# Conditioning sums of layer 0 on VectorE instead of TensorE, beside a differential attention

## The chip, the cores and the metric

The kernel runs on one core of one Trainium2 chip. The metric is the device time of one launch in microseconds. The engines are TensorE (PE; PEld is its weight load), VectorE (DVE), ScalarE (ACT), GpSimd (POOL) and the queue of SyncE (SP), which issues most transfers.

## The reference, cut to what matters

The network has two layers on 128 context tokens and 1024 latent tokens of width 1024. Layer 0 is neighbourhood attention beside differential attention, layer 1 two recurrent mixers; a SwiGLU block follows each. The change touches the modulation that every layer computes from two conditioning vectors:

```python
def ada_modulation(cond, w, b):
    m = (jax.nn.silu(cond) @ w + b)[..., None, :]
    return jnp.split(m, 6, axis=-1)

m_ctx = ada_modulation(c_ctx, w_ada[layer], b_ada[layer])
m_lat = ada_modulation(c, w_ada[layer], b_ada[layer])
h_lat = modulate(rms_norm(lat, norm_mix_g[layer]), m_lat[0], m_lat[1])
...
lat = lat + m_lat[2] * mix_lat
lat = lat + m_lat[5] * swiglu(modulate(rms_norm(lat, norm_ffn_g[layer]), m_lat[3], m_lat[4]), w_ffn_in[layer], w_ffn_out[layer])
```

So two vectors of 1024 are multiplied with a 1024 x 6144 matrix in each layer. The first two of the six parts are needed before the layer's projections, the other four only after its mixer. The work beside it in layer 0 is the differential attention:

```python
s = jnp.einsum('bqhcd,bkhcd->bhcqk', qb, k).astype(jnp.float32) * scale
p = jax.nn.softmax(s, axis=-1)
p = (p[:, :, 0] - lam * p[:, :, 1]).astype(v.dtype)
return jnp.einsum('bhqk,bkhe->bqhe', p, v)
```

## The kernel before, in words

Tokens are held as nine tiles of 128. Large products are made in three matmuls each, high part times high, high times low and low times high, from float32r halves (`split`, L73 and L74: a cast on ACT, a subtraction on DVE).

`norm_input` loads and transposes x, computes the first four 512-column groups of the modulation (`ada`, L175, float32 matmuls straight from the loaded blocks), and writes the normalized input as `hH` and `hL`. Before that last step it calls `ahead`, which opens the pool `wpool` and starts the projection of the first head group.

`attn` then has a stage for the differential attention, of four heads with nine query tiles each. `pipe` goes through the 36 units; a unit has seven pieces: `a` (load q, rope, transpose: L434 and L427 on DVE, L437 on POOL, L488), `b0` and `b1` (scores of either half, L558 and L559; row maxima on DVE, L560 and L562; exponentials on ACT, L564; sum, L568; in `b1` the combination of the halves, L581) and four pieces `c` (transposes of the probabilities, L516, copies `pT`, L518, products with V, L522). Pieces of three successive units are interleaved by the list `order`. After each piece `fill` pulls 0.28 of a step from each of two generators: `gs`, the projections of the other seven head groups (`proj_tok`, L390 to L392, result copied at L408), and `ada`, the other eight 512-column groups of layer 0's modulation.

`ada` is `ada_steps(0, range(4, 12), wpool, ps)`. A step takes one of eight blocks of 128 x 512 of a group: `ada_load` (L132, 256 KB on SP's queue, two `aw` buffers), `ada_split` (cast `awh` on ACT, L139; subtraction `awl` on POOL, L140; three buffers each) and `ada_mm` (two matmuls with the four columns of `cond`, high and low parts of both vectors, L147). Loads run three steps ahead and splits two. After eight steps `ada_end` copies the four partial rows to SBUF (L155), turns them with four small matmuls that also add high and low part (`comb`, L159), and `ada_mod` adds the bias on DVE (L169).

PSUM has eight banks. In this stage `psAB` has one `mm`, two `S`, two `T` and one `o`; `psA` has one more `S` and the bank `ada`. `_Mux` hands out score banks in the turn "bba". The `mm` bank serves the projections and the small matmuls of `ada_end`.

Layer 1's modulation is already computed in another way, by `ada_vec` beside the first SwiGLU block: DVE multiplies each block with one element per partition and accumulates into `aacc` (L221, L223), for either vector; after eight steps eight float32 matmuls with a column of ones (L229) add over the partitions, into an `mm` bank.

The order of instructions on each engine is fixed when the kernel is built: the framework's scheduler takes the program's order as priority, lets later work run ahead where its buffers are free, and places instructions by a planned timeline.

Of the kernel before, what the change touches and what calls it, by code (L numbers as in the profile page):

```python
# [12 lines left out]
F32R = mybir.dt.float32r  # L13
I32 = mybir.dt.int32
AF = mybir.ActivationFunctionType
ALU = mybir.AluOpType
AX = mybir.AxisListType
PSUM = bass.MemoryType.PSUM
DRAM = bass.MemoryType.DRAM

P = 128
# [22 lines left out]
class Net:  # L44
# [41 lines left out]
    def setup(self, top):  # L86
        tc, nc, I = self.tc, self.nc, self.I
        self.const = top.enter_context(tc.tile_pool(name="const", bufs=1))
        self.dram = top.enter_context(tc.tile_pool(name="dram", bufs=1, space=DRAM))
        c = self.const  # L90
        self.ident = self.t(c, [P, P], tag="ident")
        nc.sync.dma_start(self.ident, I["k_ident"])
        self.ones = self.t(c, [P, 1], tag="ones")
        nc.vector.memset(self.ones, 1.0)
        self.epsc = self.t(c, [P, 1], tag="epsc")
        nc.vector.memset(self.epsc, EPS)
        self.v1 = self.t(c, [P, P], tag="v1")
        self.v2 = self.t(c, [P, 44], tag="v2")
        with tc.tile_pool(name="vst", bufs=1) as p, tc.tile_pool(name="vps", bufs=2, space=PSUM) as ps:
            r1 = self.t(p, [P, P], tag="r1")  # L100
            r2 = self.t(p, [44, P], tag="r2")
            nc.scalar.dma_start(r2[0:8], I["c_ctx"].rearrange("(r p) -> r p", p=P))
            nc.scalar.dma_start(r2[8:16], I["c"].rearrange("a (r p) -> (a r) p", p=P))
            nc.scalar.dma_start(r1[0:96], I["b_ada"].rearrange("l (r p) -> (l r) p", p=P))
            nc.scalar.dma_start(r1[96:112], I["norm_mix_g"].rearrange("l (r p) -> (l r) p", p=P))
            nc.scalar.dma_start(r1[112:128], I["norm_ffn_g"].rearrange("l (r p) -> (l r) p", p=P))
            nc.gpsimd.dma_start(r2[16:24], I["rw_w0"].rearrange("a d (r p) -> (a d r) p", p=P))
            nc.gpsimd.dma_start(r2[24:32], I["rw_a0"].rearrange("a d (r p) -> (a d r) p", p=P))
            nc.gpsimd.dma_start(r2[32:36], I["rw_k_k"].rearrange("a (r p) -> (a r) p", p=P))
            nc.gpsimd.dma_start(r2[36:40], I["rw_k_a"].rearrange("a (r p) -> (a r) p", p=P))  # L110
            nc.gpsimd.dma_start(r2[40:44], I["rw_r_k"].rearrange("a (r h) k -> (a r) (h k)", h=2))
            nc.scalar.activation(r2[0:16], r2[0:16], AF.Silu)
            pt = self.t(ps, [P, 512], tag="pt")
            nc.tensor.transpose(pt[:, 0:44], r2, self.ident[0:44, 0:44])
            nc.vector.tensor_copy(self.v2, pt[:, 0:44])
            pt = self.t(ps, [P, 512], tag="pt")
            nc.tensor.transpose(pt[:, 0:128], r1, self.ident)
            nc.vector.tensor_copy(self.v1, pt[:, 0:128])
        self.cond = self.t(c, [P, KT, 4], F32R, tag="cond")
        cv = self.v2[:, 0:16].rearrange("p (c k) -> p k c", c=2)  # L120
        self.split(self.cond[:, :, 0::2], self.cond[:, :, 1::2], cv)
        self.comb = self.t(c, [4, 2], tag="comb")
        nc.scalar.dma_start(self.comb, I["k_comb"])
        self.mod = [[None] * 6, [None] * 6]
        for l in range(2):
            for j in range(6):
                self.mod[l][j] = self.t(c, [P, KT, 2], tag=f"mod{l}{j}")
# [4 lines left out]
        self.nc.sync.dma_start(w, src[:, k : k + n, cg * 512 : (cg + 1) * 512])  # L132
        return w

    def ada_split(self, w, n, pool, eng=None):
        nc = self.nc
        wh = self.t(pool, [P, n, 512], F32R, tag="awh")
        wl = self.t(pool, [P, n, 512], F32R, tag="awl")
        nc.scalar.copy(wh, w)  # L139
        (eng or nc.gpsimd).tensor_tensor(wl, w, wh, op=ALU.subtract)  # L140
        return wh, wl

    def ada_mm(self, pt, k, n, ws):
        wh, wl = ws
        for i in range(n):
            for ww in (wh, wl):
                self.nc.tensor.matmul(  # L147
                    pt[0:4, :], lhsT=self.cond[:, k + i, :], rhs=ww[:, i, :], start=k + i == 0 and ww is wh, stop=k + i == KT - 1 and ww is wl
                )

    def ada_end(self, l, cg, pt, pool, ps, r=4):

        nc = self.nc
        s4 = self.t(pool, [r, 512], tag="as4", bufs=1)
        nc.scalar.copy(s4, pt[0:r, :])  # L155
        p2 = self.t(ps, [P, 512], tag="mm")
        comb = self.comb if r == 4 else self.ident[0:2, 0:2]
        for f in range(4):
            nc.tensor.matmul(p2[:, 2 * f : 2 * f + 2], lhsT=s4[:, f * P : (f + 1) * P], rhs=comb, start=True, stop=True)  # L159
        self.ada_mod(l, cg, p2)  # L160

    def ada_mod(self, l, cg, p2):
# [12 lines left out]
    def ada(self, l, cg, pool, ps, n):  # L175

        pt = self.t(ps, [P, 512], tag="mm")
        cond = self.v2[:, 0:16].rearrange("p (c k) -> p k c", c=2)
        for k in range(0, KT, n):
            w = self.ada_load(l, cg, k, n, pool)  # L180
            for i in range(k, k + n):
                self.nc.tensor.matmul(pt[0:2, :], lhsT=cond[:, i, :], rhs=w[:, i - k, :], start=i == 0, stop=i == KT - 1)
        self.ada_end(l, cg, pt, pool, ps, 2)

    def ada_steps(self, l, cgs, pool, ps, eng=None):

        seq = [(cg, k) for cg in cgs for k in range(KT)]
        raw, spl, pt = {}, {}, None
        for i in range(-3, len(seq)):
            if i + 3 < len(seq):  # L190
                raw[i + 3] = self.ada_load(l, *seq[i + 3], 1, pool)
            if 0 <= i + 2 < len(seq):
                spl[i + 2] = self.ada_split(raw.pop(i + 2), 1, pool, eng)
            if i >= 0:
                cg, k = seq[i]
                if k == 0:
                    pt = self.t(ps, [P, 512], tag="ada")
                self.ada_mm(pt, k, 1, spl.pop(i))
                if k == KT - 1:
                    self.ada_end(l, cg, pt, pool, ps)  # L200
                yield

    def ada_vec(self, l, cgs, pool):

# [1532 lines left out]
    def run(self):  # L1737
        tc, nc, I = self.tc, self.nc, self.I
        self.tail = iter(())
        with ExitStack() as top:  # L1740
            self.setup(top)
            self.qkv = [self.dram.tile([TOK, GW], F32, name=f"qkv{g}") for g in range(8)]
            self.odr = [self.dram.tile([TOK, P], F32, name=f"odr{g}") for g in range(8)]

            hp = tc.alloc_tile_pool(name="h0", bufs=1, side="right", reuse_waits="tile")
            hH, hL = self.tiles(hp, KT, "hH", F32R), self.tiles(hp, KT, "hL", F32R)
            wes = ExitStack()

            def ahead():
                wp = wes.enter_context(self.pool("wA", side="right"))  # L1750
                self.wpool = _Bufs(wp, {"wraw": 3, "wh": 9, "wl": 9, "ist": 2, "aw": 2, "awh": 3, "awl": 3})
                self.first = self.attn_in(0, hH, hL, self.wpool)
                next(self.first)

            self.norm_input(0, hH, hL, ahead)
            self.rpb_setup()
            self.diff_lam()
            xp, x, np_, hp, hH, hL = self.attn(hp, hH, hL, wes)
            self.dump("x0", x)
            self.ffn_block(0, x, hp, hH, hL, np_)  # L1760
            self.dump("x1", x)

            self.rec_setup()
            self.rec_proj(hH, hL, x, xp, np_)
            self.rec_scan(hp)
            xp, x = self.xp, self.x1
            np_, hp, hH, hL = self.rec_out(x)
            self.dump("x2", x)
            self.ffn_block(1, x, hp, hH, hL, np_)
            self.dump("x3", x)  # L1770
            xp.release()

    def attn(self, hp, hH, hL, wes):
# [20 lines left out]
        bp = _Bufs(both.enter_context(self.pool("kAB")), {"K": 2, "Q": 3, "pT": 2, "qraw": 2, "kraw": 2})  # L1794
        head = {}
        with ExitStack() as es:
            ps = _Mux(_Bufs(es.enter_context(self.pool("psA", space=PSUM)), {"S": 1, "ada": 1}), bps, ("mm", "T", "o"), {"S": "bba"})

            rp, vp, pp, op = (es.enter_context(self.pool(f"dA{i}")) for i in range(4))
            dp = _Route(_Bufs(pp, {"P": 3}), {"rm1": rp, "rm2": rp, "V": _Bufs(vp, {"V": 2}), "ob": op, "oss": op, "rs0": op, "rs1": op, "rs2": op}, bp)  # L1800
# [1 line left out]
            self.sin = self.t(rp, [P, 8, P], tag="sin")  # L1802
            nc.scalar.dma_start(self.cos, I["k_cos"].rearrange("(n p) c -> p n c", p=P))
            nc.scalar.dma_start(self.sin, I["k_sin"].rearrange("(n p) c -> p n c", p=P))
            ada = self.ada_steps(0, range(4, 12), wpool, ps)
            self.nps = _Turns(ps, ("mm", "S", "T"))
            fin(self.first)
            self.nps = ps
# [158 lines left out]
def consts():  # L1967
# [24 lines left out]
    for w in range(4):  # L1992
        for i in range(16):
# [2 lines left out]
            pat[k] = far  # L1996
            pat[k, :, cs : cs + 16] = 0.0
            sel[k, w::4, :, i] = 1.0
    comb = np.array([[1, 0], [1, 0], [0, 1], [0, 1]], f)
    i, j = np.arange(P)[:, None], np.arange(P)[None, :]  # L2000
    scan = np.stack([np.concatenate([i < j, i <= j], 1), np.concatenate([i > j, i >= j], 1)]).astype(np.int32)
    mE, mO = [], []
# [13 lines left out]
        "k_ret": ret,  # L2016
        "k_rkd": np.concatenate([P - 1 - i, i], 1).astype(f),
    }
    return {**extra, "k_comb": comb, "k_ident": ident, "k_cos": cos, "k_sin": sin, "k_namask": nam}


_INS = [
# [29 lines left out]
```

## Time and profile before

| what | value |
| --- | --- |
| median of 3 runs | 3992.53 us (3990.24 to 3998.9) |
| the profiled execution's own time | 3991.86 us |
| its span, first to last instruction | 3990.1 us |
| PE, DVE, ACT, POOL busy | 3790.7, 2169.5, 1250.4, 711.9 us |
| mean granted TensorE clock | 0.973 of full speed |

Busy time is the union of an engine's instructions. Matmuls are pipelined and their ends are modelled, so a row's duration of a matmul is longer than its distance to the next one. "Idle before" is time in which an engine had nothing to run just before the instruction named, followed by what ended it.

### The profile page before, as it was taken

What the parts mean: (1) busy time and instruction counts of PE and PEld (TensorE: products, weight loads), DVE (VectorE), ACT (ScalarE), POOL (GpSimd) and SP (SyncE); (2) the same over time, 40 slices, a digit from 0 to 9 for tenths busy, and PEclk for the clock granted to TensorE, in tenths of its full rate; (3) what the DMA queues carried; (4) which work ended last, traced back from release to release, by engine and by line L of the source; (5) the groups of instructions that cost most, each with busy time, mean ns of one, the idle gap of its engine ahead of it and who ended that gap; (6) DMA issues with size and microseconds to landing.
All of it is one profiled execution on the core that took longest, in us unless ns stands there. A gap on an engine that the chain in (4) does not pass through costs nothing.

```text
span 3990.1 us, 62872 instructions
## 1 busy us (share of the span) xinstructions
PE 3790.7 (95%) x23989; PEld 3559.6 (89%) x23989; DVE 2169.5 (54%) x5159; ACT 1250.4 (31%) x2930; POOL 711.9 (18%) x730
## 2 busy tenths in 40 slices
PE   8999997999999999998999998888888999999998
PEld 5899997999999999998989876776777999999998
DVE  5666665666454545345254656888875543343343
ACT  4555545555111111115232322233222411111112
POOL 3321202202100000012011232233322300000000
PEclk9999998999999999999999997999999999999999
DMA  6533316432222222213243434222223211111111
GB/s 203 150 105 91 95 52 163 126 85 88 67 80 64 85 64 80 69 46 116 87 129 102 163 123 142 66 70 63 64 64 103 64 38 45 41 37 43 43 40 53
DMA packets 378086, 339.98 MB, mean 85 GB/s; under 512 B 65428, under 2 KB 328720, under 8 KB 376248
## 3 DMA queue, kind: packets, MB, share of 16 engines
q1 hardware_dynamic: 359344, 324.37, 27.0%
q10 hardware_dynamic: 13160, 7.27, 0.7%
q0 software_dynamic: 5280, 4.31, 0.5%
q8 instruction: 190, 3.11, 0.3%
q14 instruction: 112, 0.92, 0.1%
HBM read 263.37 MB, written 72.38 MB: 84 GB/s over the span
## 4 chain that ended last, share of the span: by engine, by line
PE 78%; DVE 10%; DMA 5%; issue 3%; ACT 2%; POOL 1%; SPq 0%; ACTq 0%; DVEq 0%; POOLq 0%
PE mm L81 17%; PE mm L83 17%; PE mm L82 17%; PE o L522 3%; PE mm L390 2%; PE mm L392 2%; PE mm L391 2%; PE T L516 1%; DVE MB L1241 1%; DVE tf L1240 1%; PE mm L857 1%; PE A L1190 1%; PE mm L859 1%; PE mm L858 1%; PE S L558 1%
## 5 line engine op out<-in xcount | busy, mean ns | idle before, releaser
L81 PE MATMUL mm<-hH,wh 128*128 128x384 f32 x2544 | 865.1, 341 | 20.2 <-DVE nv L363 12.6
L82 PE MATMUL mm<-hL,wh 128*128 128x384 f32 x2544 | 860.6, 339 | 2.5 <-DVE hL L366 2.5
L83 PE MATMUL mm<-hH,wl 128*128 128x384 f32 x2544 | 859.8, 339 | 0.0
L769 DVE SCALAR_TENSOR_TENSOR x<-mm,mod,x 128x384 f32<-128x384 f32 (+2 forms) x896 | 431.5, 512 | 197.5 <-PE mm L83 195.8
L81 PEld LDWEIGHTS mm<-hH,wh 128*128 128x128 f32 x2544 | 480.0, 189 | 31.4 <-ACT wh L73 18.8
L82 PEld LDWEIGHTS mm<-hL,wh 128*128 128x128 f32 x2544 | 480.1, 189 | 5.6 <-DVE hL L366 2.7
L83 PEld LDWEIGHTS mm<-hH,wl 128*128 128x128 f32 x2544 | 480.0, 189 | 4.0 <-issue 2.9
L1692 POOL TENSOR_TENSOR gl<-fs,gh 128x384 fp32r<-128x384 f32 x132 | 140.4, 1063 | 1484.1 <-ACT gh L1691 1484.1
L74 DVE TENSOR_TENSOR wl<-wraw,wh 128x512 fp32r<-128x512 f32 (+2 forms) x360 | 217.9, 618 | 336.0 <-ACT wh L73 306.4
L82 PE MATMUL mm<-gl,owh 128*128 128x384 f32 x1056 | 353.0, 334 | 0.0
L83 PE MATMUL mm<-gh,owl 128*128 128x384 f32 x1056 | 352.9, 334 | 0.0
L81 PE MATMUL mm<-gh,owh 128*128 128x384 f32 x1056 | 350.4, 335 | 0.0
L1690 DVE TENSOR_TENSOR fs<-fs,mm 128x384 f32<-128x384 f32 x132 | 73.0, 553 | 430.3 <-PE mm L83 424.7
L73 ACT CAST wh<-wraw 128x512 fp32r<-128x512 f32 (+2 forms) x360 | 188.2, 530 | 205.5 <-DMA wraw<-in_w_ffn_in_dram 77.3
L73 ACT CAST owh<-owraw 128x1024 fp32r<-128x1024 f32 x60 | 62.9, 1049 | 489.7 <-PE mm L82 446.0
L390 PE MATMUL mm<-wh,hH 128*128 128x384 f32 x576 | 199.3, 346 | 3.8 <-ACT ist L408 3.7
L82 PEld LDWEIGHTS mm<-gl,owh 128*128 128x128 f32 x1056 | 198.3, 188 | 0.1
L83 PEld LDWEIGHTS mm<-gh,owl 128*128 128x128 f32 x1056 | 198.2, 188 | 0.0
L81 PEld LDWEIGHTS mm<-gh,owh 128*128 128x128 f32 x1056 | 197.8, 188 | 0.3 <-DVE x L769 0.3
L391 PE MATMUL mm<-wl,hH 128*128 128x384 f32 x576 | 195.3, 339 | 0.0
L392 PE MATMUL mm<-wh,hL 128*128 128x384 f32 x576 | 194.0, 338 | 0.0
L1689 ACT ACTIVATE fs<-mm 128x384 f32<-128x384 f32 x132 | 64.9, 492 | 383.5 <-PE mm L83 383.4
(385 smaller groups left out, 7437.8 us busy)
## 6 DMA issues: line engine op xcount, KB each, us to landing
wraw<-in_w_ffn_in_dram SPq DMA_DIRECT2D x352, 128.0 KB
aw<-in_w_ada_dram SPq DMA_DIRECT2D x160, 256.0 KB
owraw<-in_w_ffn_out_dram SPq DMA_DIRECT2D x44, 512.0 KB
F<-stg SPq DMA_DIRECT2D x34, 640.0 KB
stg<-st SPq DMA_DIRECT2D x12, 1536.0 KB
qkv<-ist SPq DMA_DIRECT2D x72, 192.0 KB
wraw<-in_w_in_attn_dram SPq DMA_DIRECT2D x64, 192.0 KB
nab<-rpbd SPq DMA_DIRECT2D x64, 192.0 KB
```

Of the source, the lines that this page charges most:

```text
L73: nc.scalar.copy(hi, src)
L74: nc.vector.tensor_tensor(lo, src, hi, op=ALU.subtract)
L81: mm(out, lhsT=wh, rhs=xh, start=first, stop=False)
L82: mm(out, lhsT=wh, rhs=xl, start=False, stop=False)
L83: mm(out, lhsT=wl, rhs=xh, start=False, stop=last)
L390: mm(pt[:, :ncol], lhsT=hH[k][:, c], rhs=WH[k], start=k == 0, stop=False)
L391: mm(pt[:, :ncol], lhsT=hH[k][:, c], rhs=WL[k], start=False, stop=False)
L392: mm(pt[:, :ncol], lhsT=hL[k][:, c], rhs=WH[k], start=False, stop=k == KT - 1)
L522: nc.tensor.matmul(o, lhsT=pT[:, i * P : (i + 1) * P], rhs=vs(b + i), start=b + i == 0, stop=b + i == nk - 1)
L769: self.nc.vector.scalar_tensor_tensor(x[f][:, c], pt[:, a:b], self.mod[l][jg][:, f, cd : cd + 1], x[f][:, c], op0=ALU.mult, op1=ALU.add)
L1690: nc.vector.tensor_tensor(s, s, pg[1][:, :GW], op=ALU.mult)
L1692: nc.gpsimd.tensor_tensor(gl[:, sl], s, gh[:, sl], op=ALU.subtract)
```

## The change

The eight later groups of layer 0 go through `ada_vec`, as layer 1's do: two DVE operations per block, then eight float32 matmuls with the column of ones per group. `ada_split`, `ada_mm`, `ada_steps`, `cond` and `comb` are gone, with the buffers `awh`, `awl` and the bank `ada`; that bank becomes a second `S` bank of `psA`, and score banks are handed out in the turn "ba", four in rotation. `ada_end` keeps only its form for two rows, which `norm_input` uses. The pulls of 0.28 and the order list stay.

```diff
-        self.cond = self.t(c, [P, KT, 4], F32R, tag="cond")
-        cv = self.v2[:, 0:16].rearrange("p (c k) -> p k c", c=2)
-        self.split(self.cond[:, :, 0::2], self.cond[:, :, 1::2], cv)
-        self.comb = self.t(c, [4, 2], tag="comb")
-        nc.scalar.dma_start(self.comb, I["k_comb"])
...
-    def ada_split(self, w, n, pool, eng=None):
...
-    def ada_mm(self, pt, k, n, ws):
...
-    def ada_end(self, l, cg, pt, pool, ps, r=4):
+    def ada_end(self, l, cg, pt, pool, ps):
...
-    def ada_steps(self, l, cgs, pool, ps, eng=None):
...
-                self.wpool = _Bufs(wp, {"wraw": 3, "wh": 9, "wl": 9, "ist": 2, "aw": 2, "awh": 3, "awl": 3})
+                self.wpool = _Bufs(wp, {"wraw": 3, "wh": 9, "wl": 9, "ist": 2, "aw": 2})
...
-            ps = _Mux(_Bufs(es.enter_context(self.pool("psA", space=PSUM)), {"S": 1, "ada": 1}), bps, ("mm", "T", "o"), {"S": "bba"})
+            ps = _Mux(_Bufs(es.enter_context(self.pool("psA", space=PSUM)), {"S": 2}), bps, ("mm", "T", "o"), {"S": "ba"})
...
-            ada = self.ada_steps(0, range(4, 12), wpool, ps)
+            ada = self.ada_vec(0, range(4, 12), wpool)
```

The function that takes over, unchanged:

```python
    def ada_vec(self, l, cgs, pool):
        nc = self.nc
        seq = [(cg, k) for cg in cgs for k in range(KT)]
        raw, acc = {}, None
        for i in range(-1, len(seq)):
            if i + 1 < len(seq):
                raw[i + 1] = self.ada_load(l, *seq[i + 1], 1, pool)
            if i < 0:
                continue
            cg, k = seq[i]
            w = raw.pop(i)[:, 0, :]
            if k == 0:
                acc = self.t(pool, [P, 2, 512], tag="aacc", bufs=1)
            for c in range(2):
                s = self.v2[:, c * 8 + k : c * 8 + k + 1]
                if k == 0:
                    nc.vector.tensor_scalar_mul(acc[:, c, :], w, s)
                else:
                    nc.vector.scalar_tensor_tensor(acc[:, c, :], w, s, acc[:, c, :], op0=ALU.mult, op1=ALU.add)
            if k == KT - 1:
                p2 = self.t(self.nps, [P, 512], tag="mm")
                for f in range(4):
                    for c in range(2):
                        o = p2[:, 2 * f + c : 2 * f + c + 1]
                        nc.tensor.matmul(o, lhsT=acc[:, c, f * P : (f + 1) * P], rhs=self.ones, start=True, stop=True)
                self.ada_mod(l, cg, p2)
            yield
```

## Rows read from the trace of the kernel before

**Rows 1.** The page's first part: busy time, share of the span, instructions.

```profile
PE 3790.7 (95%) x23989; PEld 3559.6 (89%) x23989; DVE 2169.5 (54%) x5159; ACT 1250.4 (31%) x2930; POOL 711.9 (18%) x730
```

**Rows 2.** Table by stage: length, PE, PEld, DVE, ACT, POOL busy (instructions), clock, DMA share, GB/s.

```profile
100.00:505.00 405.00, 392.77 (x2476) 368.07 (x2475) 257.33 (x618) 220.13 (x652) 107.83 (x94) 0.99 0.37 109
505.00:600.00 95.00, 94.55 (x628) 93.07 (x627) 59.24 (x162) 43.25 (x146) 3.23 (x7) 1.00 0.17 54
600.00:700.00 100.00, 77.23 (x483) 70.00 (x481) 48.88 (x143) 53.10 (x143) 21.89 (x32) 0.81 0.64 164
```

**Rows 3.** Groups from 100 to 505 us: busy us, mean ns, idle before and releaser.

```profile
L140 POOL TENSOR_TENSOR awl<-aw,awh 128x512 fp32r<-128x512 f32 x61 | 85.6, 1412 | 121.0 <-ACT awh L139 102.0 <-PE ada L147 18.8
...
L139 ACT CAST awh<-aw 128x512 fp32r<-128x512 f32 x61 | 37.5, 623 | 41.2 <-DMA aw<-in_w_ada_dram 38.6 <-PE ada L147 2.5
...
L147 PE MATMUL ada<-awh,cond 128*4 128x512 f32 x64 | 25.6, 399 | 0.7 <-ACT as L155 0.6 <-ACT awh L139 0.2
L147 PE MATMUL ada<-awl,cond 128*4 128x512 f32 x64 | 25.5, 398 | 1.8 <-POOL awl L140 1.8
...
L437 POOL TENSOR_TENSOR rm<-rm,rm 128x128 f32<-128x128 f32 (+1 forms) x33 | 22.7, 687 | 194.6 <-DVE rm L427 117.8 <-ACT P L564 34.0 <-PE mm L392 21.0
```

**Rows 4.** Table by stretch of L139 alone: length, ACT busy (casts), clock, DMA.

```profile
328.00:352.00 24.00, 4.98 (x8) 1.00 0.47 130
352.00:397.00 45.00, 0.00 (x0) 1.00 0.26 77
```

**Rows 5.** Waits, 100 to 505 us: total us, times, longest us.

```profile
DVE sm L568 <- ACT P L564: 58.1, 39, 5.0
...
ACT awh L139 <- DMA aw<-in_w_ada_dram: 38.6, 25, 3.2
```

**Rows 6.** Timeline near 350 us: start, duration, instruction, idle before and releaser.

```profile
346.86 0.62 ACT L139 CAST awh<-aw 128x512 fp32r<-128x512 f32 x1 [3.18 <-DMA aw<-in_w_ada_dram]
...
349.21 0.16 DVE L568 TENSOR_REDUCE sm<-mx 128x1 f32<-128x3 f32 x1 [2.38 <-ACT P L564]
...
349.93 1.40 DVE L581 SCALAR_TENSOR_TENSOR P<-P,r,P 128x1152 f32<-128x1152 f32 x1
...
351.38 0.66 PE L516 MATMUL T<-ident,P 128*128 128x128 f32 x4 [1.10 <-DVE P L581]
```

**Rows 7.** Timeline of PE near 281 us: first of three matmuls, and their successor.

```profile
281.02 0.40 PE L147 MATMUL ada<-awh,cond 128*4 128x512 f32 x1
...
281.72 0.60 PE L516 MATMUL T<-ident,P 128*128 128x128 f32 x4
```

**Rows 8.** Timeline of PE: one closing group of `ada_end`.

```profile
267.81 1.05 PE L159 MATMUL mm<-comb,as 4*128 4x2 f32 x8
```

**Rows 9.** Timeline of PE in layer 1's modulation: one closing group.

```profile
1021.36 1.84 PE L229 MATMUL mm<-ones,aacc 128*128 128x1 f32 x16
```

**Rows 10.** Timeline of DVE in layer 1's modulation: one pair of sums.

```profile
985.96 1.40 DVE L223 SCALAR_TENSOR_TENSOR aacc<-aw,v,aacc 128x512 f32<-128x512 f32 x2
```

**Rows 11.** Groups of DVE by shape, 100 to 505 us.

```profile
L581 DVE SCALAR_TENSOR_TENSOR P<-P,r,P 128x1152 f32<-128x1152 f32 x24 | 37.2, 1549 | 0.0
L74 DVE TENSOR_TENSOR wl<-wraw,wh 128x384 fp32r<-128x384 f32 x48 | 32.4, 687 | 8.9 <-ACT wh L73 8.7
```

**Rows 12.** Groups of DVE by shape, 505 to 600 us.

```profile
L581 DVE SCALAR_TENSOR_TENSOR P<-P,r,P 128x1152 f32<-128x1152 f32 x7 | 9.8, 1400 | 0.0
...
L74 DVE TENSOR_TENSOR wl<-wraw,wh 128x384 fp32r<-128x384 f32 x7 | 3.7, 555 | 1.0 <-ACT wh L73 0.9
```

**Rows 13.** Layer 1's `aacc`: what DVE waited for before its sums (us, times).

```profile
  DMA aw<-in_w_ada_dram: 31.1, 29
```

**Rows 14.** Table by stretch near the start; columns as in rows 2.

```profile
40.00:50.00 10.00, 7.00 (x19) 2.01 (x20) 6.99 (x19) 7.08 (x14) 2.73 (x3) 0.83 1.04 336
...
80.00:90.00 10.00, 8.83 (x52) 8.51 (x51) 1.29 (x2) 3.21 (x5) 0.00 (x0) 1.00 0.30 90
```

**Rows 15.** Timeline of PE: the first projection matmul.

```profile
63.13 0.44 PE L390 MATMUL mm<-wh,hH 128*128 128x384 f32 x1
```

More of the change, by code (lines that the diff above doesn't have):

```diff
@@ L133, in ada_load @@
         return w
-    def ada_split(self, w, n, pool, eng=None):
+    def ada_end(self, l, cg, pt, pool, ps):
         nc = self.nc
[L137 to L141, printed above, removed]
-    def ada_mm(self, pt, k, n, ws):
[L144 to L149, printed above, removed]
-    def ada_end(self, l, cg, pt, pool, ps, r=4):
-        nc = self.nc
-        s4 = self.t(pool, [r, 512], tag="as4", bufs=1)
-        nc.scalar.copy(s4, pt[0:r, :])
+        s2 = self.t(pool, [2, 512], tag="as2", bufs=1)
+        nc.scalar.copy(s2, pt[0:2, :])
         p2 = self.t(ps, [P, 512], tag="mm")
-        comb = self.comb if r == 4 else self.ident[0:2, 0:2]
+        comb = self.ident[0:2, 0:2]
         for f in range(4):
-            nc.tensor.matmul(p2[:, 2 * f : 2 * f + 2], lhsT=s4[:, f * P : (f + 1) * P], rhs=comb, start=True, stop=True)
+            nc.tensor.matmul(p2[:, 2 * f : 2 * f + 2], lhsT=s2[:, f * P : (f + 1) * P], rhs=comb, start=True, stop=True)
         self.ada_mod(l, cg, p2)
@@ L182, in ada @@
                 self.nc.tensor.matmul(pt[0:2, :], lhsT=cond[:, i, :], rhs=w[:, i - k, :], start=i == 0, stop=i == KT - 1)
-        self.ada_end(l, cg, pt, pool, ps, 2)
-    def ada_steps(self, l, cgs, pool, ps, eng=None):
[L187 to L201, printed above, removed]
+        self.ada_end(l, cg, pt, pool, ps)
     def ada_vec(self, l, cgs, pool):
@@ L1998, in consts @@
             sel[k, w::4, :, i] = 1.0
-    comb = np.array([[1, 0], [1, 0], [0, 1], [0, 1]], f)
     i, j = np.arange(P)[:, None], np.arange(P)[None, :]
@@ L2018, in consts @@
     }
-    return {**extra, "k_comb": comb, "k_ident": ident, "k_cos": cos, "k_sin": sin, "k_namask": nam}
+    return {**extra, "k_ident": ident, "k_cos": cos, "k_sin": sin, "k_namask": nam}
 _INS = [
```

## Prediction

> **What bounds the kernel now.** I read the page first, then a table by stage, then the groups of the stage that the change touches, then single instructions. The page's busy line is the first thing to see: TensorE (PE) holds 95% of the span [rows 1], so work taken off PE can pay and work put on another engine costs only where PE comes to wait for it. By stage, the differential attention runs from about 100 to 600 us. Between 100 and 505 us, where all the PE work of `ada_steps` lies, PE is busy 392.77 of 405 us while VectorE (DVE) is busy 257.33 (64%), ScalarE (ACT) 220 and GpSimd (POOL) 108; to 600 us PE stays at 94.55 of 95 [rows 2]. So PE sets this stage. The reader should keep two numbers: PE has 12.2 us without work in the 405, DVE has 147.7.
>
> The groups show what `ada_steps` costs there: 128 matmuls on PE, 61 of its 64 casts on ACT, and as many subtractions on POOL (85.6 us) [rows 3]. The casts come in runs of eight, one run for each 512-column group, with stretches between them that hold none, the longest of 45 us: the scheduler lets a group run ahead as soon as its buffers are free [rows 4]. In such a run ACT often stands still for the next `aw` block: 38.6 us in all [rows 5]. One such wait can be followed to PE: ACT idles 3.18 us for `aw`, its exponentials come late, DVE waits 2.38 us for their sum, then combines for 1.40 us, and PE idles 1.10 us before it can transpose [rows 6].
>
> **The change, part by part.**
>
> PE, removed: 128 matmuls of 512 columns. Their recorded durations overlap; start to start, three of them take 281.72 - 281.02 = 0.70 us [rows 7], so 0.233 us each and 29.9 us together. Also removed are the eight closing groups that transpose the four partial rows, 1.05 us each [rows 8]: 8.4 us.
>
> PE, added: per group eight float32 products of a 128x128 block with the column of ones. Layer 1 does the same already: 16 instructions in 1.84 us [rows 9], so 8 x 1.84 = 14.7 us. PE net: -29.9 - 8.4 + 14.7 = **-23.6 us**, all of it in the stage that PE sets.
>
> DVE, added: 64 steps of two operations. In layer 1 a pair takes 1.40 us [rows 10]; 64 x 1.40 = 89.6 us. DVE, relieved: with POOL's subtractions gone, some DVE operations shorten. After 505 us, when POOL is nearly idle, the 1152-wide combine takes 1400 ns and the weight split 555, against 1549 and 687 between 100 and 505 [rows 11, 12]: 24 x 0.149 + 48 x 0.132 = 9.9 us. DVE then has 257.3 - 9.9 + 89.6 = 337 us of work in a stage of 405 - 23.6 = 381.4 us, 88%. It fits, because DVE's idle 147.7 us is larger than the 79.7 us net that come in, but this cover is what the whole gain hangs on. If it fails, the full price is the first rival's.
>
> The Trainium skill speaks against this placement (SBUF — State Buffer, "Who interferes with whom"): a VectorE instruction with two SBUF inputs and a GpSimd instruction that reads SBUF block each other fully. The rows above agree in direction, and the new sums have two SBUF inputs. By that rule they could also wait for POOL's rope additions, 22.7 us in this stretch [rows 3], which would make DVE's share 360 of 381 us at the very most. No run here shows yet how much of this comes about, and the sum goes by the pair as measured.
>
> ACT loses the casts (37.5 us in this stretch) and POOL all of its subtractions. Neither sets the stage, so I count nothing, except that ACT's waits for `aw` go.
>
> The wait that moves. An `aw` load is still one step ahead of its use with two buffers, but now DVE stands for it, and DVE works in order: behind it wait the row maxima of the scores, the sum of the exponentials, the combine and half of the `pT` copies, and PE waits for those. In layer 1 DVE idled 31.1 us in 96 steps for this [rows 13]; 64 steps make 20.7 us. How much reaches PE? Today ACT waits 38.6 us for the same loads and PE's whole idle time is 12.2 us, so at most 12.2/38.6 = 0.32 passes on: 6.6 us. The bounds are -12.2 us (PE's present idle time was all due to ACT and POOL, and disappears) and +20.7 us (every DVE wait reaches PE). I take +6.6, nearest to how such waits behave now, and credit nothing for ACT's waits, as DVE at 88% will queue more.
>
> The closing matmuls wait for the last sum and, as today, take the one `mm` bank; the next projection waits for DVE's bias addition. A group's sums run far ahead of its turn for that bank [rows 4], so I count nothing; if a group came late, each would cost a pair, 1.4 us, eight times 11 us. This is inside the upper bound.
>
> The bank: scores get four buffers instead of three. PE's waits for a score bank are part of its 12.2 us, so it is worth between 0 and 12.2 us, inside the lower bound just named; I take 0, as the chain followed above waits for `aw` and not for a bank. Setup loses a split and a small transfer beside the input loads: 0.
>
> The start. Before, run-ahead into the norm's stage ended with five blocks, three in `awh` and `awl` and two in `aw`, because the matmuls needed a PSUM bank; now the sums need no PSUM and a whole group of eight with two more loads can run ahead. Between 40 and 50 us the DMA engines are full at 336 GB/s [rows 14]; five more blocks of 256 KB take 1.28 MB / 336 GB/s = 3.8 us if they stand ahead of the norm's own loads, and nothing if they fall in 80 to 90 us, where DVE is busy 1.29 of 10 us. I take 0, bounds 0 to +3.8.
>
> Sum: -23.6 + 6.6 = -17.0 us. The profiled execution took 3991.86 us, 0.7 under the runs' median of 3992.53 and inside their spread, so the forecast is 3991.86 - 17.0 = **3975 us** (-0.4%). No change means within 0.2%, 8 us, about what a measurement of this kernel can tell.
>
> **The rivals.**
>
> *DVE becomes the bound (slower).* What speaks for it: 88% share, in-order waits that more work cannot fill (58.1 us for the sums of the exponentials [rows 5]) and 20.7 us for `aw`. If these all remain, DVE needs 337 + 79 = 416 us, 11 us over today's 405: 4003 us. It decides from 381 - 337 = 44 us of remaining idle time on, and makes the kernel slower from 68. Against it: the scheduler fills present waits with sums that are ready, and these come eight groups in 500 us.
>
> *The freed PE time is spent waiting (no change).* PE's 97% is built from ends that are modelled. Weight loads are busy only 368 of 405 us [rows 2]: if the 37 us between are real waits of the attention's own chain, that chain sets the stage, and 24 us less matmuls buy nothing: 3984 to 4000 us, about 3990. Against it: in the single instructions the matmuls follow each other without a gap [rows 7]. The Trainium skill (Perfetto Trace Analysis, "Identifying the Most-Contended Engine") sides with this rival: matmul occupancy is no good measure of headroom, it says, and names weight-load occupancy among the better ones.
>
> *More than the matmuls.* ACT's and POOL's late blocks were the cause of PE's idle time and DVE's waits do not reach it: -23.6 - 12.2 = -35.8, 3956 us. For it: the chain of [rows 6]. Against it: the transfer's latency stays and moves to a fuller engine.
>
> **How the numbers follow.** Forecast 0.57 (own range 3960 to 3986), waiting 0.18, DVE bound 0.13, more 0.12. Faster by over 0.2%: 0.54 of the forecast and all of "more", 0.66. Slower: the DVE bound, 0.13. Same: the rest, 0.21. The range is 3956 (the fast bound) to 3998 (short of the DVE bound's 4003): under 2 in 10 lie outside.
>
> **What would show it.** Right: the PE table for this stage shortens to about 388 us with PE still above 95%, DVE near 85 to 90%, POOL under 30 us; pairs of sums at 1.4 us in runs of eight pairs; closing groups at 1.8 us. Wrong: PE idle over 25 us with DVE's row maxima or combine as the releaser, or DVE idle for `aw` above 40 us. An end of the stage that moves by less than the PE work removed would speak for the second rival; a first projection matmul later than at 63.13 us [rows 15] would show the start's price. A different time after 600 us would be outside this argument.

## The result, and the profile after

The changed kernel took 3968.12 us (median of four runs), the kernel before 3991.39 us beside it: a ratio of 0.9934 [0.9914, 0.9953]. One of the four, 5514 us at a mean granted clock of 0.61, is not in the ratio; the median of the other three is 3966.95 us. The profiled execution took 3966.95 us with a span of 3965.1, against 3991.86 and 3990.1 before. That is 25 us less; the forecast was 17 less, and the time lies inside its range. The trace shows that most of it did not come from where the forecast put it.

First the steps that can be checked at their place. The page's busy line after the change, beside [rows 1]:

```profile
PE 3762.7 (95%) x23925; PEld 3541.0 (89%) x23925; DVE 2220.7 (56%) x5286; ACT 1212.7 (31%) x2857; POOL 619.1 (16%) x666
```

The table by stage, columns as in [rows 2]:

```profile
100.00:480.00 380.00, 366.67 (x2340) 350.92 (x2340) 279.93 (x679) 174.81 (x548) 21.46 (x31) 1.00 0.37 110
480.00:576.00 96.00, 94.09 (x633) 92.14 (x633) 72.61 (x190) 48.75 (x159) 5.96 (x9) 1.00 0.23 69
```

The groups of DVE from 100 to 480 us, which answer to [rows 10, 11], and one closing group on PE, which answers to [rows 9]:

```profile
L184 DVE SCALAR_TENSOR_TENSOR aacc<-aw,v,aacc 128x512 f32<-128x512 f32 x84 | 61.2, 759 | 9.6 <-DMA aw<-in_w_ada_dram 9.5
L542 DVE SCALAR_TENSOR_TENSOR P<-P,r,P 128x1152 f32<-128x1152 f32 x22 | 30.8, 1401 | 0.0
L74 DVE TENSOR_TENSOR wl<-wraw,wh 128x384 fp32r<-128x384 f32 x48 | 27.4, 586 | 7.7 <-ACT wh L73 7.7
...
368.35 1.95 PE L190 MATMUL mm<-ones,aacc 128*128 128x1 f32 x16 [0.57 <-ACT ist L369]
```

PE is still at 96% of its stage. POOL is down to 21 us. The combine fell from 1549 to 1401 ns and the weight split from 687 to 586, about as forecast. All 128 operations of the sums together took 12.28 us before 100 us, 66.47 from 100 to 480 and 10.96 after: 89.7 us, where the forecast had 89.6. DVE waited 9.5 us for `aw` in this stretch and 11.9 us in all, a little over half of the 20.7 assumed.

Now where the 25 us came from. I cut both traces at first and last instructions: the first projection matmul, the last product of the differential attention (`o<-V,pT`), the first matmul of layer 0's feed-forward block, the first and last `A<-AR,BK` of the recurrent scan, and the last gate product of the scan's output behind it (`mm<-sg,gup`). Some 20 us of output projection behind that last cut count with the second feed-forward block. Two of these cuts in the trace of the changed kernel (operation, count: duration ns min/median/max, first and last start):

```profile
L351 PE MATMUL mm<-wh,hH x576: 331/334/525, 63.4 to 594.3; 128*128 128x384 f32 x192
...
L81 PE MATMUL mm<-hH,wh x32: 334/334/522, 957.4 to 976.9; 128*128 128x384 f32 x32
...
L1151 PE MATMUL A<-AR,BK x576: 376/376/793, 2388.2 to 2922.3; 64*128 64x256 f32 x192
```

and the scan in the kernel before:

```profile
L1190 PE MATMUL A<-AR,BK x576: 376/376/793, 2390.2 to 2935.3; 64*128 64x256 f32 x192
```

| stretch, us | before | after | difference |
|---|---|---|---|
| to the first projection | 63.1 | 63.4 | +0.3 |
| differential attention | 563.9 | 555.9 | -8.0 |
| neighborhood attention, output projection | 333.7 | 338.1 | +4.4 |
| first feed-forward, projections of layer 1 | 1429.5 | 1430.8 | +1.3 |
| scan | 545.1 | 534.2 | -10.9 |
| output of the scan | 169.4 | 169.2 | -0.2 |
| second feed-forward block | 885.4 | 873.6 | -11.8 |

The stage that the change touches gave 8.0 us, and with the neighborhood attention behind it only 3.6. The other 22.7 us appeared in the scan and in the second feed-forward block, whose code the change does not touch.

I call the attention and what follows it up to the first feed-forward matmul, 897.6 us before and 894.0 after, the mixer. To see PE's side of it, I took every matmul of the differential attention from start to start of its successor. Up to the median of its kind (same tiles, same shape) this time is counted as work, and what is over the median as waiting. Work went from 518.1 to 494.4 us: -23.7, where the forecast had -23.6. Waiting went from 45.8 to 61.5 us: +15.7, where it had +6.6. The split depends on the measure: with number times median as the work it is -21.8 and +13.8.

A part of that waiting can be read at the start. Rows of the changed kernel's timeline from 58 to 85 us, DVE and POOL first, then PE:

```profile
60.86 2.14 DVE L184 SCALAR_TENSOR_TENSOR aacc<-aw,v,aacc 128x512 f32<-128x512 f32 x2
61.02 1.43 POOL L262 TENSOR_TENSOR hL<-xn,hH 128x384 fp32r<-128x384 f32 x1 [0.30 <-DVE xn L259]
...
73.64 7.19 DVE L259 TENSOR_SCALAR xn<-xn,mod,mod 128x256 f32<-128x256 f32 x12
80.75 2.14 DVE L184 SCALAR_TENSOR_TENSOR aacc<-aw,v,aacc 128x512 f32<-128x512 f32 x2
82.81 2.89 DVE L262 TENSOR_TENSOR hL<-xn,hH 128x384 fp32r<-128x384 f32 x6
...
83.41 0.69 PE L353 MATMUL mm<-wh,hL 128*128 128x384 f32 x1 [4.57 <-DVE hL L262]
83.89 0.53 PE L351 MATMUL mm<-wh,hH 128*128 128x384 f32 x1
84.21 0.53 PE L352 MATMUL mm<-wl,hH 128*128 128x384 f32 x1
```

Eight pairs of sums ran on a DVE that the norm still filled. The last pair stood ahead of the block of `hL` that PE wanted, PE stood for 4.57 us, and then its matmuls started 0.32 us apart. In the kernel before PE's longest stand near here was 1.17 us. The granted clock says why the matmuls were slow; the table by stretch (columns as above) against 1.00 in [rows 14]:

```profile
80.00:90.00 10.00, 6.59 (x22) 6.59 (x23) 6.99 (x12) 0.50 (x2) 1.65 (x2) 0.66 0.22 67
90.00:100.00 10.00, 10.00 (x59) 10.00 (x58) 0.89 (x4) 3.89 (x8) 0.00 (x0) 1.00 0.29 89
```

The pair of 2.14 us at 60.86 ran while POOL subtracted for `hL`, and so did the last pair; the usual pair takes 1.40 [rows 10]. That is the direction of the rule that the prediction cited from the Trainium skill (SBUF — State Buffer, "Who interferes with whom"), and over the whole stage it mattered little: 759 ns on average for a sum.

### The profile page after: what moved, and what is told of

Read it like the earlier page. It is cut to its first block, busy times and chain, and to the rows that moved or that the text cites. A ratio compares the mean times of both kernels' runs of the same rounds, so it can differ in the third digit from the quotient of the medians.

```text
span 3965.1 us, 62683 instructions
## 1 busy us (share of the span) xinstructions
PE 3762.7 (95%) x23925; PEld 3541.0 (89%) x23925; DVE 2220.7 (56%) x5286; ACT 1212.7 (31%) x2857; POOL 619.1 (16%) x666
## 4 chain that ended last, share of the span: by engine, by line
PE 76%; DVE 11%; DMA 7%; issue 2%; ACT 2%; SPq 0%; POOL 0%; DVEq 0%; ACTq 0%; POOLq 0%
PE mm L81 17%; PE mm L83 17%; PE mm L82 17%; PE o L483 3%; PE mm L351 2%; PE mm L353 2%; PE mm L352 2%; PE mm L818 1%; PE mm L819 1%; PE mm L820 1%; PE T L477 1%; DVE tf L1201 1%; DVE MB L1202 1%; PE A L1151 1%; DVE aacc L184 1%
## 5 line engine op out<-in xcount | busy, mean ns | idle before, releaser
L74 DVE TENSOR_TENSOR wl<-wraw,wh 128x512 fp32r<-128x512 f32 (+2 forms) x360 | 210.1, 596 | 333.7 <-ACT wh L73 304.4
L184 DVE SCALAR_TENSOR_TENSOR aacc<-aw,v,aacc 128x512 f32<-128x512 f32 x280 | 208.2, 776 | 42.5 <-DMA aw<-in_w_ada_dram 42.1
```

Source lines behind the costliest of these rows:

```text
L74: nc.vector.tensor_tensor(lo, src, hi, op=ALU.subtract)
L184: nc.vector.scalar_tensor_tensor(acc[:, c, :], w, s, acc[:, c, :], op0=ALU.mult, op1=ALU.add)
```

## The experiments

Twelve kernels ran. This table has what the argument uses: lengths in us from one profiled execution of each, cut as above, the median of its runs, and the ratio to the kernel before with its 95% interval.

| kernel | attention | mixer | scan | second feed-forward | runs, median | ratio |
|---|---|---|---|---|---|---|
| before_again | 566.8 | 897.8 | 538.6 | 884.3 | 3988.48 | 0.9998 [0.998, 1.0016] |
| before_pad32 | 569.5 | 903.8 | 545.0 | 883.2 | 3993.71 | 1.0015 [1.0004, 1.0025] |
| before_shift160 | 570.1 | 908.2 | 547.7 | 874.5 | 3985.8 | 0.9994 [0.998, 1.0009] |
| again | 553.2 | 890.6 | 535.1 | 873.6 | 3964.33 | 0.9947 [0.9928, 0.9965] |
| after_pad32 | 558.5 | 897.1 | 528.3 | 874.9 | 3966.65 | 0.9946 [0.9929, 0.9963] |
| late_pool | 555.4 | 890.9 | 533.1 | 875.4 | 3964.52 | 0.9941 [0.9922, 0.9959] |
| three_banks | 567.9 | 893.6 | 545.7 | 874.0 | 3983.79 | 0.9974 [0.9961, 0.9988] |
| one_vector | 549.5 | 883.7 | 539.8 | 876.0 | 3961.58 | 0.993 [0.9909, 0.995] |
| late_start | 555.9 | 893.9 | 539.2 | 875.2 | 3978.21 | 0.9972 [0.9956, 0.9989] |
| no_sums | 530.8 | 862.9 | 536.2 | 874.8 | 3948.46 | 0.9907 [0.9882, 0.9931] |
| act_pool | 571.6 | 902.3 | 545.0 | 875.1 | 3994.03 | 1.0013 [0.9999, 1.0027] |
| act_pool_late | 572.9 | 906.8 | 543.3 | 875.1 | 3990.27 | 1.0007 [0.9991, 1.0023] |

**again and before_again** repeat the two kernels unchanged.

> The changed kernel once more, for the repeatability of its stages. Both theories expect the median near 3967 us, the norm's end with PE waiting some 4.6 us for hL near 83 us, the last product of the differential attention near 619 us, and the second SwiGLU block's matmuls 173.4 ns apart. If the two late stages (scan and second SwiGLU block), which no edit touched, change from execution to execution, their 22 us would be chance: then they differ here by several us from the first profile.

> The kernel before once more, for the repeatability of its late stages. If the late gain belongs to the kernels, the second SwiGLU block's matmuls are again some 175.5 ns apart and the scan takes about 545 us; if it is chance between executions, they fall to 173.4 ns or 534 us in this one.

The result holds: 0.9947. The same program's mixer came out at 894.0 and 890.6 us, its scan at 534.2 and 535.1 after and 545.1 and 538.6 before, its second feed-forward block within 1.1 us. A difference of a few us in one stretch of one profile is therefore no finding, except in the last block.

**The second feed-forward block: before_pad32, after_pad32, before_shift160.** Both kernels issue the same matmuls there in the same order, but for 16 of the first 47. But the change takes two small tiles out of the constant pool, and every tile that lies behind them on that side moves by 160 bytes. The pads put 32 bytes into that pool of the one or the other kernel:

```
             nc.vector.tensor_copy(self.v1, pt[:, 0:128])
...
+        self.pad = self.t(c, [P, 8], tag="pad")
+        nc.gpsimd.memset(self.pad, 0.0)
```

> The kernel before with the same 32 unused bytes, all matmuls and sums as before. Placement theory: second SwiGLU block 10 us shorter, 3981 us; with the scan's part 3969 us. Theory of the forecast and theory of the order: no change, 3991 us.

> The changed kernel with 32 unused bytes per partition in the constant pool: every tile of the left side moves by 32 bytes, the order on PE, DVE, ACT and SP stays. Placement theory (the second SwiGLU block became faster because the left side now has the same remainder modulo 64 as the right side): the remainder is wrong again, its matmuls go back from 173.4 to about 175.6 ns, +10 us, 3977 us; if the scan's 12 us are placement too, 3989 us. Theory of the forecast (all the gain is matmuls removed in layer 0) and the theory that the scheduler's order made the late gains: no change, 3967 us.

before_shift160 is the kernel before with its two tiles `cond` and `comb` moved to the weight pool, so that the rest moves by the 160 bytes and no instruction of the change is made:

```
+    def cond_setup(self, c):
+        nc, I = self.nc, self.I
         self.cond = self.t(c, [P, KT, 4], F32R, tag="cond")
...
                 next(self.first)
+                self.cond_setup(self.wpool)
```

> The kernel before with its four conditioning columns and their combining matrix in the pool of the projection weights instead of the constants: every left-side tile gets exactly the address of the changed kernel (160 bytes lower), all arithmetic stays on its engines. Address theory: the scan falls from 545 to about 534 us and the second SwiGLU block's matmuls from 175.5 to 173.4 ns, together some 20 us, 3970 us. Theory of the schedule (the late gain comes with other instruction streams, not with addresses): no change, 3991 us. Theory of the forecast: no change either, but then the changed kernel's late stages stay unexplained.

The table from 3200 to 3900 us, where nothing but this block runs, in the kernel before, the changed kernel and before_shift160 (columns as in [rows 2]; the count behind PE is the number to read):

```profile
3200.00:3900.00 700.00, 700.00 (x3988) 700.00 (x3987) 249.15 (x445) 118.31 (x201) 57.59 (x54) 1.00 0.14 42
```

```profile
3200.00:3900.00 700.00, 700.00 (x4040) 700.00 (x4039) 244.75 (x438) 121.96 (x208) 60.15 (x57) 1.00 0.14 41
```

```profile
3200.00:3900.00 700.00, 700.00 (x4040) 700.00 (x4039) 257.25 (x464) 117.28 (x200) 58.16 (x55) 1.00 0.14 42
```

PE is full in all three at the full clock, and it starts a matmul every 700/3988 = 175.5 ns before, and every 700/4040 = 173.3 ns in both others. The block takes 883.2 to 885.4 us in the three profiles with the old addresses or 32 bytes more, and 873.6 to 876.0 us in the eleven with a shift of 128 or 160 bytes, whatever else these kernels change. The 11 us are an effect of where tiles lie. 160 bytes in the kernel before turned it. 32 bytes in either kernel did not, which speaks against the remainder modulo 64 that both expectations named; in the kernel before they moved the count from 3988 to 4000. Which tile and which property of its address decides stays open. before_shift160 got no faster overall: its mixer, in which instructions were issued in another order, took 10 us longer, and its scan did not fall to 534 us as expected.

**late_pool, late_start: the start.** The first attempt gave the sums' tiles the memory of the norm's input tiles, so that they could not start before these were done.

```
-                self.wpool = _Bufs(wp, {"wraw": 3, "wh": 9, "wl": 9, "ist": 2, "aw": 2})
+                self.wpool = _Bufs(wp, {"wraw": 3, "wh": 9, "wl": 9, "ist": 2})
...
-            ada = self.ada_vec(0, range(4, 12), wpool)
+            ada = self.ada_vec(0, range(4, 12), _Bufs(es.enter_context(self.pool("dA4")), {"aw": 2}))
```

> The changed kernel with the blocks and sums of layer 0 in a pool that opens with the attention stage, on memory that the norm's stage uses, so that no sum can run before the norm is done. Theory that the start lost 6 to 8 us because eleven pairs of sums ran on a full DVE: PE's wait for hL near 83 us goes, the first projections come as early as before, 3960 us. Rival (the first group's sums cost as much in the attention stage, where DVE is at three quarters): 3967 us.

A miss: that memory was free by 31 us, the sums still ran from 39 us on, and PE's 4.57 us wait stayed. late_start ties them to the norm's end by data:

```
-                s = self.v2[:, c * 8 + k : c * 8 + k + 1]
+                s = (self.v2 if l else self.late)[:, c * 8 + k : c * 8 + k + 1]
...
+            self.late = self.t(rp, [P, 16], tag="late")
+            nc.vector.scalar_tensor_tensor(self.late, hL[7][:, TOK - 16 : TOK], 0.0, self.v2[:, 0:16], op0=ALU.mult, op1=ALU.add)
```

> The changed kernel, with one edit: layer 0's sums read their scalars from a copy that is made after the last block of hL, so that no sum can run while the first norm still needs VectorE. Theory (the start costs because eight pairs of sums stand ahead of the norm's last operations on a full VectorE): PE's wait of 4.57 us for hL at 83 us goes, the projections at 88 to 106 us come some 6 to 8 us earlier, and from the first projection to the first FFN product of layer 0 the kernel needs 885 to 888 us instead of 890.6 to 894.0; the kernel takes 3957 to 3961 us. Rival (the sums only move to a VectorE that is as full later): the same sum of 890 to 894 us, and a time within 3 us of the changed kernel's 3964 to 3968.

Two rows of its trace, from PE's timeline and from the table by stretch:

```profile
82.01 0.44 PE L351 MATMUL mm<-wh,hH 128*128 128x384 f32 x1 [2.19 <-ACT ist L369]
...
80.00:100.00 20.00, 17.99 (x95) 17.99 (x96) 12.46 (x23) 4.57 (x9) 0.00 (x0) 0.91 0.60 176
```

The wait for `hL` is gone. A shorter one of 2.19 us for ACT is left, and with it a part of the low clock. Up to 100 us PE waited 4.9 us less than in the changed kernel (3.0 less than in again). Then it paid back: 6.6 us more between 500 and 600 (3.7 more than in again). Attention and mixer are the changed kernel's to 0.1 us. The rival was right about the mixer: the sums have to be made somewhere, and the first norm was no worse a place than the end. Its runs were even some 10 us slower than the changed kernel's, with an equal mixer; that leads to the scan, below.

**one_vector, no_sums: what the sums cost.** one_vector makes the sums of one vector only and uses them for both, with all loads:

```
-            for c in range(2):
+            for c in range(2 if l else 1):
...
-                        nc.tensor.matmul(o, lhsT=acc[:, c, f * P : (f + 1) * P], rhs=self.ones, start=True, stop=True)
+                        nc.tensor.matmul(o, lhsT=acc[:, c if l else 0, f * P : (f + 1) * P], rhs=self.ones, start=True, stop=True)
```

> The changed kernel with layer 0's later sums made for the first vector alone and used for both: half of DVE's added work, 45 us, is left out, PE's work and the transfers stay, and the outputs are not the reference's. Theory that DVE's load costs PE the 15 us that the attention stage fell short of the removed matmuls: the stage shortens from 555.9 towards 545 us, PE's waits shrink by 7 us or more, 3958 us. Rival (the waits come from the attention's own chain and from transfers): less than 3 us, 3965 us.

no_sums keeps one step of eight in each group:

```
-            if i + 1 < len(seq):
+            if i + 1 < len(seq) and (l or seq[i + 1][1] == 0):
...
-            for c in range(2):
+            for c in range(2 if l or k == 0 else 0):
```

> The changed kernel, with seven of eight steps of layer 0's later conditioning left out, loads and sums (each group has only its first pair); the output is therefore not the reference's. The closing groups on PE and the fourth score bank stay. Theory (VectorE's queue is what the missing gain was paid to): from the first projection to the first FFN product 873 to 877 us, which is the 897.7 of before less the forecast net of 23.6 us of PE work, or a few us more if the new order of the neighborhood attention costs by itself; the kernel 3944 to 3952 us. Rival (the attention's own chain sets the stage, and PE's freed time cannot be used): no less than the 883.7 us of the run with half of the sums; the kernel 3956 us or more. The scan and the second FFN block should stay as in the changed kernel, the scan at 528 to 535 us if its order is that of the changed kernel and at 538 to 548 us if it is that of the kernel before.

The table by stage of no_sums:

```profile
100.00:480.00 380.00, 372.82 (x2457) 365.93 (x2456) 247.41 (x648) 187.56 (x593) 23.36 (x34) 1.00 0.27 80
```

2457 matmuls fit into these 380 us, against 2340 in the changed kernel. With the same measure as above the attention's work on PE is 493.5 us and its waiting 37.3, against 45.8 and 48.6 in the two profiles of the kernel before, 54.6 with half of the sums and 58.8 to 61.5 with all of them. So three things can be set apart in the attention: PE's own work, -23.7; less waiting for all else that differs, 37.3 less 45.8 to 48.6, so -8.5 to -11.3; and the sums with their loads, +21.5 to +24.2. The middle term holds the blocks that ScalarE and GpSimd no longer handle, but the fourth score bank as well, which three_banks puts at 10.2 us of waiting with the sums in place. No run sets the two apart. The second rival is out: without the sums PE's freed time is used in full and the mixer takes 862.9 us, 10 us below the theory's range, which knew nothing of the middle term. The price is not in proportion to DVE's time: the first half of the sums with most of the loads costs 54.6 - 37.3 = 17.3 us, the second half 4 to 7. one_vector fell between its two expectations: a mixer of 883.7 us, 7 to 10 less than with all sums, and 3961.58 us where 3958 and 3965 were named.

**act_pool, act_pool_late: other engines for half of the sums.** ScalarE multiplies the second vector's block, GpSimd adds it up; act_pool_late has late_start's edit as well.

```
-                if k == 0:
+                if c and not l:
+                    u = acc[:, 1, :] if k == 0 else self.t(pool, [P, 512], tag="au")
+                    nc.scalar.activation(u, w, AF.Copy, scale=s)
+                    if k:
+                        nc.gpsimd.tensor_tensor(acc[:, 1, :], acc[:, 1, :], u, op=ALU.add)
+                elif k == 0:
```

> The changed kernel, with layer 0's sums of the second vector taken from VectorE: ScalarE multiplies the block by its scalar (64 times some 0.6 us, the price of its cast of the same shape before) and GpSimd adds it to the sum (56 times some 1.4 us, the price of its subtraction of the same shape before). Theory (VectorE's load is what costs): like the run with half of the sums left out, 884 us from the first projection to the first FFN product, 8 us less than the changed kernel; the kernel some 3957 to 3961 us. Rival 1 (ScalarE's in-order queue feels the blocks as it did before, and GpSimd slows VectorE): no less than 890 us and a time within 3 us of the changed kernel. Rival 2 (the other engines are worse): above 895 us, 3969 us or more.

> Both edits together: VectorE's sums (first vector) start after the norm's last block, the second vector's go over ScalarE and GpSimd; of these the scalars too are those of the late copy. If both edits act and their gains add, 879 to 882 us from the first projection to the first FFN product, and 3951 to 3956 us for the kernel. If the start is the same loss that half the sums already avoid, as act_pool alone, within 2 us. If neither acts, the changed kernel's time.

Both lost, at 3994.03 and 3990.27 us, the second rival's case. In act_pool, what ScalarE waits for from 60 to 576 us (us, times, longest), and the sums of the first vector, left on DVE, from 90 to 625 us:

```profile
ACT au L183 <- DMA aw<-in_w_ada_dram: 58.1, 30, 9.5
...
L189 DVE SCALAR_TENSOR_TENSOR aacc<-aw,v,aacc 128x512 f32<-128x512 f32 x49 | 50.7, 1035 | 9.4 <-DMA aw<-in_w_ada_dram 9.2
```

ScalarE stands for the blocks again, more than in [rows 5], with the exponentials and the drains of PE's banks behind it. And DVE was hardly unloaded: beside GpSimd's additions a sum took 1035 ns instead of 759, and DVE's busy time from 100 to 480 us is 272.01 us, against 279.93 in the changed kernel and 258.79 in one_vector. PE's waiting in the attention is 77.0 us, 22.4 more than with these sums simply left out. How much of this is ScalarE's wait and how much the slower DVE, the two runs do not tell.

**three_banks: the score bank.** The changed kernel with the three score buffers of before:

```
-            ps = _Mux(_Bufs(es.enter_context(self.pool("psA", space=PSUM)), {"S": 2}), bps, ("mm", "T", "o"), {"S": "ba"})
+            ps = _Mux(_Bufs(es.enter_context(self.pool("psA", space=PSUM)), {"S": 1}), bps, ("mm", "T", "o"), {"S": "bba"})
```

> The changed kernel with three score banks in the old turn; the freed bank stays unused. Forecast (the bank is worth nothing): attention stage 555.9 us as in the changed kernel, 3967 us. Rival (the fourth bank pays for part of DVE's load): the stage is 5 us or more longer, 3972 us or more.

The attention took 12 us longer than in the changed kernel, PE's waiting in it 10.2 us more, and the neighborhood attention was 12 us shorter: a mixer of 893.6 us, the same. The fourth bank moves waiting from one stage to the next. Its runs were 16 to 19 us slower than the changed kernel's all the same, and the scan is 11.5 us longer.

**The scan.** None of these kernels changes its code. Compared instruction by instruction, the traces hold two orders of it: the changed kernel, again, after_pad32 and late_pool share one; the kernel before and all the others share the other, but for a few instructions (of the scan's 3624 matmuls 1689 stand elsewhere in the one than in the other, and no kernel of the second group differs from the kernel before in more than 72). The four profiles of the first order take 528.3 to 535.1 us, the ten of the second 536.2 to 547.7. In late_start, with the changed kernel's mixer, the scan is 5.0 us longer and its output 3.6 us, and the runs are slower by some 10 us. The addresses are not the cause: seven of the ten have those of the changed kernel or near them, and take 536.2 to 547.7 us. The run medians agree: with the difference in mixer taken off, an estimate from one profile each, these seven lie 4 to 18 us, 11 on average, above the changed kernel. So the order is the likeliest cause of some 10 us on average (means 532.7 and 542.6); but the ranges nearly touch, one program varies by 6.5 us, and the old order was not run in an otherwise unchanged kernel. It is argued, not shown.

## Why the prediction was right, and where it was not

The total was right, and in good part by luck: 22.7 of the 25 us came from stages that the forecast left out. The end of the attention moved by 8.0 us where 23.6 us of PE work had gone, which the prediction itself had named as a sign for its second rival.

- *PE's net of -23.6 us* was right: -23.7 by starts, with closing groups of 1.95 us and every other matmul near its old price. It was also usable, as no_sums shows. (One of the eight old closing groups ran at 554 us, behind the stretch in which the prediction saw them all.)
- *DVE's 89.6 us* was right to 0.1 us. Its share was not: 74% instead of 88%. 23.2 us of the sums ran before 100 or after 480 us, and the relief was larger: by the groups of both traces from 90 to 625 us, combine and split lost 8.2 us (forecast 9.9), but the rope's operations and others lost another 12, the 128x128 products with `cos`, for one, going from 356 to 288 ns.
- *The wait that moves, +6.6 us*, is the term that was mis-sized. I expected DVE's waiting for `aw`, passed on to PE at a third. DVE waited 11.9 us only, and PE's waiting still grew by 10.2 to 15.7 us over the two profiles of either kernel. Behind this net stand -8.5 to -11.3 us from ScalarE, GpSimd and the bank together, where I credited nothing inside a bound of -12.2, and +21.5 to +24.2 us from the sums with their loads, above my upper bound of +20.7. That bound counted only the time for which DVE stands. What it left out, I think, is the time for which an in-order DVE is busy with a sum while a row maximum, a split of weights or a block of `hL` that PE needs stands behind it. This was read at its place for `hL` alone; for the rest the runs show the price and not the path.
- *The start at 0* was wrong. I looked at the DMA engines and at 80 to 90 us, where DVE was idle before, and took the first projection matmul as the sign. It came at 63.4 us, as before; the loss came 20 us later, at the last block of `hL`, and cost 7.7 us more waiting up to 100 us (5.8 in the repeat). Moving it away won nothing, though, so it is a place where the sums' price is paid and not a price of its own.
- *The bank at 0* agrees with the mixer of three_banks, one profile; within the attention it was worth 12 us.
- *After 600 us* the prediction named nothing. 11.8 us came with the addresses of tiles and 10.9 from the scan, most likely by its order; the neighborhood attention gave back 4.4. Without these, the change would have been worth the mixer's 4 to 7 us: no change by the bound of 0.2%.
- *The rivals.* DVE did not become the bound: its idle time, 100 of 380 us, is far above the 44 us at which that case began. The second rival's number for the mixer was close (nothing gained) and its mechanism wrong: by occupancy of the weight loads, 91% before and 92% after, PE looked stuck, yet no_sums reaches 365.93 of 380 us, 96%. "More than the matmuls" is what no_sums shows, and the sums took it away.

No version that makes the whole computation beat the changed kernel.

## What to carry to other kernels

Here the work that left the bounding engine was gained in full, and 21 to 24 us of it were paid back in waiting for the in-order engine that took it, although a quarter of that engine was free. So price also the time that urgent work may stand behind the new work, not only the free share and the loads. Before a gain is put down to a change, cut both traces at the same instructions and see in which stage it lies; 23 of 25 us here lay where nothing had been edited. And when a tile is added or removed, compare the spacing of matmuls in stages far away, since a shift of addresses alone moved it here.

## What the runs showed of the hardware

- Back-to-back 128x128 by 384 matmuls, PE full, granted clock 1.00, started every 175.5 ns with one placement of tiles and every 173.3 ns with another, 160 bytes lower: 11 us over 885. 32 bytes more in the kernel before gave 175.0 ns (4000 in 700 us).
- After PE had stood for 4.57 us at 79 to 83 us, its matmuls started 0.32 us apart instead of 0.17, at a granted clock of 0.66 over 10 us: the lower level, 1.2 GHz, for a part of these, and 2.4 GHz again from 90 us on. In late_start PE stood for 2.19 us, and 0.7 us later its matmuls were 0.32 us apart as well.
- A pair of sums on DVE took 2.14 us beside a subtraction on GpSimd, and 1.40 without. With sums on GpSimd as well (act_pool), one on DVE took 1035 ns on average, against 759.
